# Loading keys and the first queries three gate sets earlier in a hybrid decoder layer

## The chip, the cores and the metric

The kernel runs on one core of a Trainium2 chip. The core has a matrix engine (TensorE, in the profile PE, its weight loads PEld), a vector engine (VectorE, DVE), a scalar engine (ScalarE, ACT), a general engine (GpSimd, POOL) and a synchronising engine (SyncE, SP), which here issues nearly all DMA transfers. Each engine works through its own list of instructions in order and waits by semaphores for the others. The metric is the device time of one execution in microseconds (us); lower is better.

## The reference, cut to what matters

One decoder layer over 1024 tokens of width 1024 in float32: a SwiGLU block, a mixer and a second SwiGLU block. The change lies in the mixer:

```python
proj = u @ w_in[l]
(nq, nkc, nvc, nks, nvs, nkw, nvw, ngt, rq, rk, rv, rg, ga, gb) = jnp.split(proj, split_pts, axis=-1)
o_nsa = nsa_attention(nq..., nkc, nvc, nks, nvs, nkw, nvw, jax.nn.sigmoid(ngt)..., cmp_k_pe[l], cmp_k_w1[l], ...)
o_ret = retention(rq..., rk..., rv..., pos)
...
mixed = jax.nn.sigmoid(ga) * y_nsa + jax.nn.sigmoid(gb) * y_ret
# inside nsa_attention: kc = compress(k_cmp, ...), vc = compress(v_cmp, ...); for every head
# softmax of q @ kc (compressed), q @ k_slc (selected) and q @ k_win (window), each times its values, summed by gates
def compress(raw, pe, w1, w2):
    ...
    return jax.nn.silu(flat @ w1) @ w2
```

So there are projections of the normed input `u` (queries, keys, values, two wide gates `ga` and `gb`), a small network that compresses keys and values, a recurrent "retention", and an attention with three branches.

## The kernel before, in words

**Precision.** Every float32 operand of a matmul is split into a high part (a cast on ACT) and a low part (a subtraction on DVE), and a product is three matmuls (`mm3`).

**Projections.** The wide projections are taken two column blocks at a time as a "set" (`set_t`): `wset` (lines 321 to 348) loads two weight tiles `raw` of 512 KB, called a and b here, into the pool `W`, which holds **three** `raw` tiles in this stage; GpSimd forms sums and differences S of them (lines 341 to 344), ACT and DVE split them into `wp` (lines 334 and 335), and `seven` (line 380) runs seven products of 12 matmuls of 128x512 (line 281). The moving operands of the seven products are, in this order, u0, u0, T2, T3, T4, u1, u1 (in the profile u0h/u0l, t2h/t2l and so on), tiles of the pool `sp`. The results are added on DVE (lines 395 to 416), and for the gates ACT applies the sigmoid (line 1453) and SP stores them in DRAM (`d_gab`).

There are eleven such sets in `sets()`: keys (to `d_k`), two of queries (to `d_q`, one slab for each of four pairs of heads), and eight gate sets, called gate set 0 to gate set 7 below. They are one generator, `fill`, woven in the program into the retention core, the compression and the key loading. A planner of the tile framework then orders the instructions of each engine by its own costs, so that the order in the program is a wish, not the result.

**Compression** (`compress`, lines 822 to 879) runs for keys and then for values. For each: DMA of the raw rows into `kst`, the weights `w1` and the position rows `pe`; a transpose of `pe` (line 840); its copy (842); a chain of 16 dependent DVE instructions on `pea` (844, 846); one small matmul (848) and the copy of its result as bias (851); 16 matmuls over `kst` (855, 32 records in the trace); the activation `hid` (859); a second small matmul (873 for the values); and the splits into `v2c` (878, 879). `kst` is one place, so the rows of the values come when the matmuls of the keys are done.

**Keys and queries.** `keys` (line 1010) loads `d_k` back in four parts, each two DMAs of 256 KB (line 1020) into a stage tile that is one of the **same three** `raw` tiles, and splits it into `Kh` (ACT, line 1022) and `Kl` (DVE, line 1023). These live in a pool `kv`, which takes the room of the pool that the compression used. `queries(p)` does the same with `d_q[p]` in two halves (lines 1048, 1049, 1050). The queries of pair 0 go to the place `t3h`, which the moving operand T3 of the sets has until the last set's fourth product; those of pair 1 go to `t3l`, over a stage tile `t4h` that lies where T4 was.

**Attention** (line 1067). For each pair and each block of 128 queries PE makes score tiles (lines 1063 and 1064), DVE adds the mask and takes the row minimum (1110 to 1122), ACT takes the exponential (1125), GpSimd scales (1130), and so on.

The program's order around the change, in `run`, is: last of the retention, compression woven with four steps of `fill` for each of its own, then `fill` up to the mark "late", then `keys` with two steps of `fill` after each part, then the rest of `fill`, then queries of pair 0, values, queries of pair 1, attention.

Of the kernel before, what the change touches and what calls it, by code (L numbers as in the profile page):

```python
# [10 lines left out]
F32R = mybir.dt.float32r  # L11
# [6 lines left out]
P = 128  # L18
T = 1024
D = 1024  # L20
KD = D // P
# [12 lines left out]
def drain(*gens):  # L34
    for g in gens:
        for _ in g:
            pass


def weave(main, fill, n):  # L40

    done = 0
    for i, _ in enumerate(main, 1):
        while done < i * n:
            next(fill, None)
            done += 1


def f32(ap):
    return ap.bitcast(F32)  # L50


class Layer:
# [953 lines left out]
    def stage(self):  # L1007
        return self.W.tile([P, 2, H2], F32, name="raw", bufs=self.wr)
# [30 lines left out]
    def queries(self, p, pool, stage):  # L1039
        nc = self.nc  # L1040
        src = self.d_q[p].rearrange("(j d) t -> d j t", j=2)
        Q = self.Q[p] = pool.tile([P, 2, T], F32R, name="t3" + "hl"[p % 2])
        lr = slice(64, 128) if p < 2 else slice(0, 64)
        for hf in (1, 0):
            s = slice(hf * H2, (hf + 1) * H2)
            a = stage()
            for r in range(2):
                nc.sync.dma_start(a[64 * r:64 * r + 64], src[:, :, s])
            nc.scalar.copy(Q[:, :, s], a)
            nc.vector.tensor_sub(Q[lr, :, s], a[lr], f32(Q[lr, :, s]))  # L1050

    def scores(self, ps, h, b, i, k0, kn, off):

        nc = self.nc
        g = h // 4
        e = slice(i * P, (i + 1) * P)
        q = self.Q[h // 2][:, h % 2, e]
        a = off
        while a < off + kn:
            z = min(off + kn, (a // H2 + 1) * H2)  # L1060
            ks = slice(k0 + a - off, k0 + z - off)
            kh, kl = (self.kch, self.kcl) if b == 2 else (self.Kh[b], self.Kl[b])
            nc.tensor.matmul(ps[:, a:z], q, kh[:, g, ks], start=True, stop=False)  # L1063
            nc.tensor.matmul(ps[:, a:z], q, kl[:, g, ks], start=False, stop=True)  # L1064
            a = z

    def attention(self, pool, sp, stage, psS, psT, psO, fill):
# [7 lines left out]
        for p in range(4):  # L1075
            g = p // 2
            for i in range(NT - 1, -1, -1):
                if p and p < 3 and i == 7:
                    self.queries(p + 1, sp, stage)
                elif i in FILL[p]:  # L1080
                    next(fill, None)
                late = p == 3 and i < 4
# [205 lines left out]
    def run(self):  # L1288
# [6 lines left out]
        def pool(ctx, name, side="left"):  # L1295
            return ctx.enter_context(tc.tile_pool(name=name, bufs=1, side=side, reuse_waits="tile"))

        def psum(ctx, name, bufs):
            return ctx.enter_context(tc.tile_pool(name=name, bufs=bufs, space=PSUM, reuse_waits="tile"))
# [133 lines left out]
        sp = pool(c_n, "sevenm", "right")  # L1433
# [12 lines left out]
        def to(dst):  # L1446
            def sink(n, hf, t):
                nc.sync.dma_start(dst[n][:, hf * H2:(hf + 1) * H2], t)
            return sink

        def to_gate(d):
            def sink(n, hf, t):
                nc.scalar.activation(t, t, AF.Sigmoid)
                nc.sync.dma_start(self.d_gab[d + (KD if n == "b" else 0), :, hf * H2:(hf + 1) * H2], t)
            return sink
# [19 lines left out]
        def sets():  # L1475
            yield from self.set_t(self.w_in, 768, 1024, us, sp, to({"a": self.d_k[0], "b": self.d_k[1]}))
            for p in (0, 2):
                yield from self.set_t(self.w_in, p * P, (p + 1) * P, us, sp, to({"a": self.d_q[p], "b": self.d_q[p + 1]}))
            for d in range(KD):
                if d == KD - 1:  # L1480
                    yield "late"
                yield from self.set_t(self.w_in, 3352 + d * P, 4376 + d * P, us, sp, to_gate(d))

        drain(sets_ret(0))
        more = sets_ret(1)
        fill = itertools.chain(more, sets())
        for r in range(2):
            with ExitStack() as c1:
# [4 lines left out]
        kv = pool(c_n, "kv", "right")  # L1493
        for x in fill:
            if x == "late":
                break
        weave(self.keys(kv), fill, 2)
        drain(fill)


        c_ps.close()
        c_a = ExitStack()
        psT, psS, psO = psum(c_a, "psT", 3), psum(c_a, "psS", 4), psum(c_a, "psOT", 1)
        self.Q = {}
        self.queries(0, sp, self.stage)
        self.values(sp, self.stage)
        self.c_w.close()

        def stage():
            return sp.tile([P, 2, H2], F32, name="t4h")  # L1510
        att = pool(c_a, "att")
        self.queries(1, sp, stage)
        onsa = self.attention(att, sp, stage, psS, psT, psO, self.ret_up(sp, stage, psS))
        c_a.close()
        c_n.close()
# [76 lines left out]
```

## Time and profile before

| | us |
|---|---|
| Three runs | 2452.97, 2454.83, 2447.19; median 2452.97 |
| The profiled execution | 2450.27, of which span of the trace 2448.5 |
| Gate set 6 begins on PE | 1223.98 |
| Last matmul of gate set 7 starts | 1271.63 |
| First score tile reduced on DVE | 1283.81 |
| First exponential of the attention on ACT | 1289.90 |
| Mean granted clock of TensorE | 0.967 of full speed |

The times within the span count from its start. A row of the list of instructions in order of time gives the start, the duration, the engine, the line of the kernel, the operation and its tiles, the shape, how many instructions are merged in the row (x), and in brackets how long the engine had been idle and what released it.

### The profile page before, as it was taken

Reading aid. Unit: us, or ns where it says so; the run is one execution under the profiler, and the core shown is the slowest. Engines: PE = TensorE matmul, PEld = TensorE weight load, DVE = VectorE, ACT = ScalarE, POOL = GpSimd, SP = SyncE. Lnnn points to the kernel's source line nnn. Section 1 sums busy time; section 2 is a strip of 40 time slices with the busy share of each in tenths; the row PEclk is TensorE's granted clock in tenths of the full one; section 3 lists DMA queues with packets and bytes.
Section 4 is the critical chain, followed back from the end, with each engine's and each line's share of the span. In section 5 each row is a group of like instructions: output and inputs, shape, how many; then the busy total and the mean of one; then the engine's idle time right before and its main releaser. Section 6 shows DMA issues by size and latency. Waiting matters only on the chain.

```text
span 2448.5 us, 32717 instructions
## 1 busy us (share of the span) xinstructions
PE 2284.3 (93%) x11563; PEld 1909.0 (78%) x11563; DVE 1860.7 (76%) x2790; ACT 1031.7 (42%) x1860; POOL 1252.7 (51%) x920
## 2 busy tenths in 40 slices
PE   7799999999977999999989999988889999999997
PEld 5578888878856899888868889866668888887875
DVE  8888887578999856666668887669985555558998
ACT  5333222245744422223348776624432222235655
POOL 3855454444576545555215544456754444435366
PEclk8999999999998999999998999999889999999998
DMA  9135655263204344343551221640322222255201
GB/s 345 56 112 169 201 176 186 86 232 134 78 0 136 97 142 121 110 138 110 167 165 51 74 79 57 213 153 0 103 69 78 82 78 86 85 190 186 94 1 69
DMA packets 248888, 288.32 MB, mean 118 GB/s; under 512 B 14852, under 2 KB 169236, under 8 KB 248724
## 3 DMA queue, kind: packets, MB, share of 16 engines
q1 hardware_dynamic: 248608, 286.19, 36.6%
q8 instruction: 91, 1.49, 0.3%
q14 instruction: 73, 0.60, 0.1%
q10 hardware_dynamic: 116, 0.05, 0.0%
HBM read 216.45 MB, written 69.73 MB: 117 GB/s over the span
## 4 chain that ended last, share of the span: by engine, by line
PE 31%; DVE 12%; DMA 3%; issue 2%; ACT 1%; POOL 1%; SPq 0%; DVEq 0%; ACTq 0%; POOLq 0%
PE po L281 16%; DVE wp L678 4%; PE ot L1166 2%; DVE hT L782 2%; PE po L750 2%; PE pt L1152 2%; PE s L750 2%; PE s L281 2%; PE s L1063 1%; PE s L1064 1%; DMA tn<-d_gab 1%; PE pt L855 1%; PE ot L1163 0%; PE po L495 0%; DMA hT<-d_h 0%
## 5 line engine op out<-in xcount | busy, mean ns | idle before, releaser
L750 PE MATMUL po<-wp 128*128 128x512 f32 x1176 | 293.7, 406 | 30.2 <-DVE wp L678 27.6
L281 PE MATMUL po<-u0h,wp 128*128 128x512 f32 x944 | 305.6, 395 | 9.2 <-DVE gates L991 4.9
L750 PEld LDWEIGHTS po<-wp 128*128 128x128 f32 x1176 | 227.9, 196 | 91.2 <-DVE wp L678 38.1
L281 PE MATMUL po<-u1h,wp 128*128 128x512 f32 x880 | 281.9, 391 | 3.7 <-DVE bias L544 2.2
L750 PE MATMUL s<-wp 128*128 128x512 f32 x1008 | 247.4, 403 | 21.0 <-DVE wp L678 19.7
L750 PEld LDWEIGHTS s<-wp 128*128 128x128 f32 x1008 | 195.9, 195 | 67.3 <-DVE wp L678 24.4
L334 ACT CAST wp<-S 128x1024 fp32r<-128x1024 f32 x98 | 102.9, 1050 | 302.5 <-PE po L281 300.4
L281 PEld LDWEIGHTS po<-u0h,wp 128*128 128x128 f32 x944 | 178.9, 189 | 49.9 <-DVE gates L991 5.1
L463 POOL TENSOR_TENSOR t<-t,t 128x512 f32<-128x512 f32 x38 | 55.3, 1456 | 301.8 <-DVE t L407 191.9
L281 PEld LDWEIGHTS po<-u1h,wp 128*128 128x128 f32 x880 | 165.1, 188 | 40.5 <-DVE bias L544 2.6
L281 PE MATMUL po<-u0l,wp 128*128 128x512 f32 x472 | 185.4, 393 | 0.0
L281 PE MATMUL po<-u1l,wp 128*128 128x512 f32 x440 | 172.5, 392 | 2.6 <-DVE u1l L243 2.6
L335 DVE TENSOR_TENSOR wp<-S,wp 128x1024 fp32r<-128x1024 f32 x98 | 159.8, 1630 | 15.8 <-ACT wp L334 15.6
L334 ACT CAST wp<-raw 128x1024 fp32r<-128x1024 f32 x98 | 82.0, 837 | 186.0 <-PE po L281 174.4
L341 POOL TENSOR_TENSOR S<-raw 128x512 f32<-128x512 f32 x49 | 68.7, 1403 | 157.0 <-DMA raw<-w_in 92.2
L281 PE MATMUL po<-t2h,wp 128*128 128x512 f32 x392 | 132.2, 397 | 2.2 <-ACT t2h L300 2.1
L281 PE MATMUL po<-t3h,wp 128*128 128x512 f32 x392 | 132.1, 398 | 0.2 <-DVE t L395 0.2
L281 PE MATMUL po<-t4h,wp 128*128 128x512 f32 x392 | 131.6, 396 | 0.8 <-DVE tn L399 0.7
L395 DVE TENSOR_TENSOR t<-tn,po 128x512 f32<-128x512 f32 x57 | 39.0, 685 | 110.4 <-issue 78.7
L335 DVE TENSOR_TENSOR wp<-raw,wp 128x1024 fp32r<-128x1024 f32 x98 | 113.6, 1159 | 11.9 <-ACT wp L334 11.8
L1156 DVE TENSOR_TENSOR pl<-pt,ph 128x512 fp32r<-128x512 f32 (+2 forms) x160 | 96.9, 619 | 11.9 <-ACT ph L1155 11.1
L281 PEld LDWEIGHTS po<-u0l,wp 128*128 128x128 f32 x472 | 89.7, 190 | 18.1
(471 smaller groups left out, 6248.4 us busy)
## 6 DMA issues: line engine op xcount, KB each, us to landing
raw<-ffn_w_in SPq DMA_DIRECT2D x88, 512.0 KB, 4.8
raw<-ada_w SPq DMA_DIRECT2D x56, 512.0 KB, 4.4
raw<-w_in SPq DMA_DIRECT2D x40, 512.0 KB, 4.2
d_g<-t SPq DMA_DIRECT2D x50, 256.0 KB, 2.0
d_h<-hT SPq DMA_DIRECT2D x24, 512.0 KB, 5.8
hT<-d_h SPq DMA_DIRECT2D x48, 256.0 KB, 5.3
d_g<-tg SPq DMA_DIRECT2D x38, 256.0 KB, 2.0
fw<-ada_w SPq DMA_DIRECT2D x8, 1024.0 KB, 11.1
```

The source lines that it names most:

```text
L281: nc.tensor.matmul(ps, a, b, start=k == 0 and q == 0, stop=k == n - 1 and q == 2)
L334: nc.scalar.copy(w[:, 0], t)
L335: nc.vector.tensor_sub(w[:, 1], t, f32(w[:, 0]))
L341: nc.gpsimd.tensor_add(s[:, 0:4], b[:, 0:4], b[:, 4:8])
L395: nc.vector.tensor_add(c, u2, p)
L463: nc.gpsimd.tensor_mul(g, g, t)
L678: nc.vector.tensor_sub(w[:, x, 1], g(n[x]), f32(w[:, x, 0]))
L750: nc.tensor.matmul(po[d], l[:, e], r, start=k == 0 and z == 0 and not seeded, stop=k == m - 1 and z == 2, skip_group_check=seeded)
L782: self.nc.vector.scalar_tensor_tensor(h, po, self.ab[:, 3 * i + 2, d:d + 1], h, op0=ALU.mult, op1=ALU.add)
L1152: nc.tensor.transpose(pt[:, o + j * P:o + (j + 1) * P], a, self.ident)
L1156: nc.vector.tensor_sub(lo, pt[:, :n], f32(hi))
L1166: nc.tensor.matmul(ot, self.V2[kt // 4][:, kt % 4, b, g, :], x[:, o:o + 2 * P], start=first and m == 0, stop=last and m == 1)
```

## The change

The tile of pair 0's queries gets a name of its own, `Q0`, and is taken from the pool `kv` beside the keys. `queries` becomes a generator with a step after each half; where it was called before it is now drained. `keys` and these queries are chained and woven, two steps of `fill` each time, from a mark "late" that stands before gate set 5 instead of gate set 7.

```diff
     def queries(self, p, pool, stage):
         nc = self.nc
         src = self.d_q[p].rearrange("(j d) t -> d j t", j=2)
-        Q = self.Q[p] = pool.tile([P, 2, T], F32R, name="t3" + "hl"[p % 2])
+        Q = self.Q[p] = pool.tile([P, 2, T], F32R, name="t3" + "hl"[p % 2] if p else "Q0")
...
             nc.scalar.copy(Q[:, :, s], a)
             nc.vector.tensor_sub(Q[lr, :, s], a[lr], f32(Q[lr, :, s]))
+            yield
...
                 if p and p < 3 and i == 7:
-                    self.queries(p + 1, sp, stage)
+                    drain(self.queries(p + 1, sp, stage))
...
             for d in range(KD):
-                if d == KD - 1:
+                if d == KD - 3:
                     yield "late"
...
-        weave(self.keys(kv), fill, 2)
+        self.Q = {}
+        weave(itertools.chain(self.keys(kv), self.queries(0, kv, self.stage)), fill, 2)
         drain(fill)
...
         psT, psS, psO = psum(c_a, "psT", 3), psum(c_a, "psS", 4), psum(c_a, "psOT", 1)
-        self.Q = {}
-        self.queries(0, sp, self.stage)
         self.values(sp, self.stage)
...
-        self.queries(1, sp, stage)
+        drain(self.queries(1, sp, stage))
```

What the planner makes of it is seen in the order of the built programs. First TensorE, where gate set 5 ends (its last product is on u1). Before, gate set 6 (u0) follows at once, and the four steps of the values' compression (lines 840, 848, 855 and 873) stand far apart among the matmuls of gate sets 6 and 7:

```order
L281 MATMUL po<-u1l,wp 128x512
L281 MATMUL po<-u1h,wp 128x512
L281 MATMUL po<-u0h,wp 128x512
L281 MATMUL po<-u0l,wp 128x512
L281 MATMUL po<-u0h,wp 128x512 x2
```

Now the four stand together between gate set 5 and gate set 6:

```order
L281 MATMUL po<-u1l,wp 128x512
L281 MATMUL po<-u1h,wp 128x512
L840 MATMUL pt<-ident,pe 128x16
L848 MATMUL pt<-ones,pea 128x1
L855 MATMUL pt<-kst,w_9561 128x126 x16
L873 MATMUL pt<-w_9563,hid 64x64 x2
L281 MATMUL po<-u0h,wp 128x512
```

Nothing of gate set 6 is left ahead of them. After the two u0 products of gate set 6 come eight score matmuls of the attention's first block, then the rest of gate sets 6 and 7, then the attention.

VectorE at the same place: before, the chain of the values' compression (`pea`) is spread over gate set 6, between additions (lines 399 to 412) and weight splits (335), and the key splits (1023) come at the end of gate set 7:

```order
L844 TENSOR_SCALAR pea<-w_9561,peT 128x128
L846 SCALAR_TENSOR_TENSOR pea<-w_9561,peT,pea 128x128 x3
L399 TENSOR_TENSOR tn<-tn,po 128x512
L846 SCALAR_TENSOR_TENSOR pea<-w_9561,peT,pea 128x128 x5
L403 TENSOR_TENSOR tg<-tn,po 128x512
L846 SCALAR_TENSOR_TENSOR pea<-w_9561,peT,pea 128x128 x5
L407 TENSOR_TENSOR t_10271<-tg,po 128x512
```

Now it is one piece behind gate set 5's last addition (416), the key splits follow it, and the first weight split of gate set 6 (335) comes after all of them:

```order
L416 TENSOR_TENSOR tn<-tn,po 128x512
L842 COPY peT<-pt 128x16
L844 TENSOR_SCALAR pea<-w_9561,peT 128x128
L846 SCALAR_TENSOR_TENSOR pea<-w_9561,peT,pea 128x128 x15
L851 COPY peb<-pt 128x1
L879 TENSOR_TENSOR v2c<-pt,v2c 64x64
L1023 TENSOR_TENSOR Kl_10044<-raw,Kh_10042 128x2x512 x2
L1023 TENSOR_TENSOR Kl_10045<-raw,Kh_10043 128x2x512
L879 TENSOR_TENSOR v2c<-pt,v2c 64x64 x2
L1023 TENSOR_TENSOR Kl_10045<-raw,Kh_10043 128x2x512
L879 TENSOR_TENSOR v2c<-pt,v2c 64x64
L335 TENSOR_TENSOR wp<-raw,wp 128x1024
```

SyncE, which issues the loads: before, the two weight tiles of gate set 7 (line 327) go out between stores of the gates, and the later parts of the keys (1020) follow them:

```order
L327 DMA raw<-w_in 128x8x128
L1454 DMA d_gab<-tg 128x512
L1454 DMA d_gab<-tn 128x512
L327 DMA raw<-w_in 128x8x128
L1454 DMA d_gab<-t_10225 128x512
L1454 DMA d_gab<-t_10271 128x512
L1020 DMA raw<-d_k 64x2x512 x2
```

Now the last part of the keys goes out first, then the two weight tiles of gate set 6, then both halves of pair 0's queries (1048), then the two weight tiles of gate set 7:

```order
L1455 DMA d_gab<-tn 128x512
L1020 DMA raw<-d_k 64x2x512 x2
L327 DMA raw<-w_in 128x8x128 x2
L1048 DMA raw<-d_q 64x2x512 x4
L327 DMA raw<-w_in 128x8x128 x2
L1455 DMA d_gab<-t_10255 128x512
```

All of these go into the three `raw` places. In the built program the two weight tiles of gate set 6 take the places of the second and third parts of the keys, the last part of the keys takes the place of the first, and both halves of the queries follow in that place. The queries of pair 0 and the keys share the order on ACT: the casts of `Kh` stand behind the values' `hid` (859) and the first `v2c` (878). In the pool `kv`, which has grown by `Q0`, the high parts of the first keys now lie outside the room of the compression; their low parts lie where `kst` and the keys' `w1` were.

## Rows read from the trace of the kernel before

**Rows 1.** The page, busy time, share of the span and instructions by engine:

```profile
PE 2284.3 (93%) x11563; PEld 1909.0 (78%) x11563; DVE 1860.7 (76%) x2790; ACT 1031.7 (42%) x1860; POOL 1252.7 (51%) x920
```

**Rows 2.** TensorE in order of time, from gate set 6 into the attention:

```profile
1223.98 0.39 PE L281 MATMUL po<-u0h,wp 128*128 128x512 f32 x1
...
1242.12 0.50 PE L281 MATMUL po<-u1h,wp 128*128 128x512 f32 x1 [1.25 <-DVE t L407]
...
1244.98 0.28 PE L848 MATMUL pt<-ones,pea 128*128 128x1 f32 x2
...
1250.30 7.04 PE L855 MATMUL pt<-kst,w 128*128 128x126 f32 x32
...
1260.47 0.45 PE L873 MATMUL pt<-w,hid 128*64 128x64 f32 x4
...
1271.63 0.39 PE L281 MATMUL po<-u1h,wp 128*128 128x512 f32 x1
1273.81 0.50 PE L1063 MATMUL s<-Kh,t3h 128*128 128x512 f32 x1 [1.79 <-DVE t3h L1050]
...
1284.55 0.79 PE L1063 MATMUL s<-Kh,t3h 128*128 128x512 f32 x1 [8.96 <-DVE mx L1110]
```

**Rows 3.** Stretches of TensorE: from:to and length, busy (instructions), granted clock, DMA:

```profile
1276.00:1278.00 2.00, 0.00 (x0) 1.00 1.15 213
1278.00:1280.00 2.00, 0.00 (x0) 0.76 1.11 333
...
1290.00:1292.00 2.00, 1.38 (x4) 0.50 0.47 160
...
1296.00:1298.00 2.00, 2.00 (x13) 0.98 0.00 0
```

**Rows 4.** VectorE in order of time, both compressions, key splits and attention's start:

```profile
1189.39 1.51 DVE L846 SCALAR_TENSOR_TENSOR pea<-w,peT,pea 128x128 f32<-128x128 f32 x4
...
1224.18 0.69 DVE L416 TENSOR_TENSOR tn<-tn,po 128x512 f32<-128x512 f32 x1 [0.47 <-PE po L281]
...
1230.28 0.17 DVE L842 COPY peT<-pt 128x16 f32<-128x16 f32 x1
...
1230.97 0.28 DVE L844 TENSOR_SCALAR pea<-w,peT 128x128 f32<-128x128 f32 x1
...
1236.07 5.39 DVE L846 SCALAR_TENSOR_TENSOR pea<-w,peT,pea 128x128 f32<-128x128 f32 x5
...
1262.14 2.36 DVE L1023 TENSOR_TENSOR Kl<-raw,Kh 128x1024 fp32r<-128x1024 f32 x2 [0.73 <-ACT Kh L1022]
...
1283.81 0.68 DVE L1110 CUSTOM_DVE_ANT_0 u0h<-s,S 128x512 f32<-128x512 f32 x1
```

**Rows 5.** ScalarE in order of time, from the values' compression to the first exponential:

```profile
1257.38 0.37 ACT L859 ACTIVATE hid<-pt,peb 128x126 f32<-128x126 f32 x1 [7.25 <-PE pt L855]
...
1260.95 0.21 ACT L878 CAST v2c<-pt 64x64 fp32r<-64x64 f32 x1 [0.51 <-PE pt L873]
...
1265.41 1.05 ACT L1022 CAST Kh<-raw 128x1024 fp32r<-128x1024 f32 x1 [2.12 <-DMA raw<-d_k]
...
1287.54 1.04 ACT L1049 CAST t3l<-t4h 128x1024 fp32r<-128x1024 f32 x1 [5.28 <-DMA t4h<-d_q]
1288.60 1.28 ACT L1125 ACT_TABLE_LOAD   x1
1289.90 1.15 ACT L1125 ACTIVATE u0h<-u0h,mx 128x1024 f32<-128x1024 f32 x1
```

**Rows 6.** First key load on SP; DMA issues (count, KB, median us to landing); landing of stage t4h:

```profile
1206.05 0.65 SPq L1020 DMA_DIRECT2D raw<-d_k  x1
...
raw<-d_k SPq DMA_DIRECT2D x8, 256.0 KB, 4.5
...
raw<-w_in SPq DMA_DIRECT2D x40, 512.0 KB, 4.2
...
DMA to landing us min/median/max: 3.3/4.5/7.5
```

## The prediction

> **What bounds the kernel now.** I read the page first: TensorE is busy for 93% of the span [rows 1], so a gain has to close a hole on it or shorten what stands ahead of one. Then I read the instructions of TensorE in order of time around the place that the change touches [rows 2]. Gate sets 6 and 7 run from 1223.98 to about 1271.9 (the last matmul starts at 1271.63 and the next could follow 0.23 later). Then TensorE waits 1.79 us for pair 0's queries, makes the first four score tiles in about 1.7 us, and waits 8.96 us for VectorE, whose first score reduction is at 1283.81 [rows 2, 4]. The first exponential is at 1289.90, behind the split of pair 1's queries and a table load of 1.28 us [rows 5]. That is 18.0 us from the end of gate set 7 to the first exponential. The granted clock shows the same hole: it falls from 1.00 to 0.50 of 2.4 GHz within some 4 us of the last score tile, and is back only in the stretch from 1296 [rows 3]. This hole is what the change can win; 18 us minus what has to be done there anyway.
>
> The other thing to read is why the keys were late before. The first key load is issued at 1206.05 [rows 6], but its cast begins after 1260.95, behind the first `v2c` of the values' compression [rows 5]. So it was not the load that the keys waited for, but the compression: the places of the keys lie in its room, and on ACT their casts stand behind its `hid` and `v2c`.
>
> **The change, part by part: the compression on TensorE.** Now look at the order of the built program. Nothing of gate set 6 stands ahead of the values' compression any more, and nothing can: the weight tiles of gate set 6 take `raw` places that the second and third key parts hold, these are free only when the keys are split, the splits stand on VectorE behind `pea` and the first `v2c`, and on ACT behind `hid`. So TensorE, done with gate set 5 at 1223.98, goes through one dependent chain. I add it up from rows:
>
> 1. Last addition of gate set 5, copy, first step: 0.69 + 0.17 + 0.28 [rows 4]; then 15 steps on `pea`. These took 1.51 for 4 (0.38 each) in one place and 5.39 for 5 (1.08 each) in another [rows 4]; in the second GpSimd was forming S of the next weights. Now these weights are not loaded, GpSimd has nothing to do, so I take 0.38: 5.7. Bounds 5.7 and 16. Together 6.8.
> 2. Matmul 848, bias copy (about 0.15), 855, `hid`, 873, first `v2c`: 0.28 + 0.15 + 7.04 + 0.37 + 0.45 + 0.21 [rows 2, 5] = 8.5.
> 3. The clock: TensorE has stood for 6 us by then, longer than it stood when the clock fell [rows 3]. It was at half from the restart near 1290.6 until 1296 [rows 3], about 5 us, which is 2.5 us of work lost. I add 2.5; bounds 0 and 2.7.
> 4. Key cast 1.05, two low parts 2.36 [rows 4, 5]: 3.4. Now the place for weight tile a of gate set 6 is free.
> 5. Weight tile a: issue 0.4, landing 4.2 [rows 6], cast 1.05, thus 5.7. But the last key part takes longer, and its low part stands ahead of the weight split on VectorE: it can be issued one low part (1.2) earlier, its two issues cost about 1.2, then landing 4.5 [rows 6], cast 1.05, split 1.2, thus 6.8 from the end of step 4. Then the `v2c` split 0.2 and the weight split 1.2. Together 8.2.
>
> The sum is 29.4 us from the end of gate set 5 to the start of gate set 6. Of this, 8.0 us of TensorE work (840, 848, 855, 873) lay inside gate sets 6 and 7 before, and the wait of 1.25 us there for VectorE [rows 2], which was busy with `pea`, should go. So gate set 6 proper starts **20 us later** than it would have.
>
> **Gate sets 6 and 7.** The 14 products took (1271.9 - 1223.98 - 8.0 - 1.25) / 14 = 2.76 us each; that stays. The restart costs another 2.5 us at half clock, and the eight score matmuls that now stand inside gate set 6 cost 1.7 us. They need the first half of pair 0's queries, which goes into the place of the last key part: free at 29.4 - 1.4 = 28 after gate set 5, plus issue 1.2, landing 4.5 and two splits 2.3 = 36. TensorE gets there after 29.4 + 5.5 + 2.5 = 37.4: no wait, with 1 us to spare. The weights of gate set 7 go out behind the second half of the queries, near 38 to 42, and are wanted at about 52: covered, with 5 us to spare after the landing and the split. So gate set 7 ends near 1271.9 + 20.1 + 2.5 + 1.7 = **1296.2**, some 24 us later.
>
> **The start of the attention.** Pair 0's queries and the keys are then ready, and the 1.79 us wait and the crowd of loads (DMA share 1.11 in [rows 3]) go. What is late next is pair 1's queries: their stage `t4h` lies on T4, so their load still waits for gate set 7's fifth product, 5.5 us before the end. From there: issue 0.6, landing 4.5 [rows 6], cast 1.05, split 1.2, then the second half 0.6 + 4.5 + 1.05 (same rows), and the table load 1.28 [rows 5]: 14.8, so 9.3 us after the end of gate set 7 instead of 18.0. This gives back 8.7. The first exponential comes at 1305.5, **15.6 us later** than 1289.90. VectorE has by then reduced eight score tiles instead of five, worth about 1.5 us where it is the later one; That TensorE then works at full clock for the next 6 us I take at nothing (bounds -2 and 0), because each score tile of that stretch also waits for VectorE. Net: 24.3 - 8.7 - 1.5 = **+14 us**.
>
> **Costed at nothing.** `Q0` as a place, the `drain` calls and the steps of the generator add no instruction. The second weight tile of gate set 5 is loaded one turn later, but its split waited for a `wp` place anyway; if that cover fails it costs 1 to 3 us at gate set 5. The planner also orders the first pair of the attention anew; nothing is added there, and I give it -3 to +3.
>
> **A rule against this.** The key load issued at 1206.05 was used 55 us later [rows 5, 6]. The Trainium skill, page "DMA: Bandwidth & Descriptors", section "Rules for kernel authors", says to issue a DMA early, compute meanwhile and wait for it late, so that its fixed cost is hidden. By that rule alone loading keys and queries sooner wins the hole before the attention; here the early load holds one of three places that weights need, which the rule doesn't speak of. It is the second rival below.
>
> **The rivals.**
> - *Slower by 9 to 20 us* (forecast): the chain above.
> - *Faster*: the keys are out of the way before gate set 6 needs its places, the weights come in time, and the hole goes: 1.79 + 8.96 us and half of the slow stretch, about -13, thus 2440. For it: that is what the order in the program asks for, and the high parts of the first keys lie outside the compression's room now. Against it: ACT and VectorE have these splits behind `hid`, `v2c` and `pea` in their lists, and the low parts lie on `kst`. It would need gate set 6's weights landed within 8 us of gate set 5's end; the chain makes that 23.
> - *No difference*: the chain is right but every uncertain term is at its lower end: no clock loss twice (-5), landings at 3.3 (-3), the attention's new order at its best (-3): +3, thus 2456. It decides where the hole in TensorE is under 22 us instead of 29.
> - *Much slower*, over +20: `pea` at the slow rate (+10), or gate set 7's weights, behind two query halves on SP, late as well: their 5 us to spare is used up if each of three loads takes 2 us longer than the median; then +6 to +10. Thus 2474 to 2480.
>
> **How the numbers follow.** The sum is made against the profiled execution: 2450.27 + 14 = 2464.3. That execution is 2.7 below the median of the three runs, 2452.97, against which a new median would be held; so I predict 2467. The chances: forecast 0.70, no difference 0.13, much slower 0.09, faster 0.08. The range from 2456 to 2477 takes in the forecast, the upper part of no difference, and the lower part of much slower; about 2 in 10 is left out. About 0.3%, or 7.4 us, is what a measurement of this kernel tells from no change. Faster by more than that: 0.08; within it: 0.13 and a little of the forecast's lower end, 0.15; slower: 0.77.
>
> **What the profile of the changed kernel would show.** Right: TensorE stands for about 6 us before 848 and for 10 us or more between 873 and gate set 6; 855 and the start of gate set 6 run at a clock of 0.50; the last matmul of gate set 7 starts near 1296; the first exponential comes about 9 us after it, behind the split of pair 1's queries. Wrong: gate set 6 beginning before 1245, key splits ahead of 855, or a wait at gate set 7's first product. The prediction falls if the hole ahead of gate set 6 is less than 15 us, or if the attention gains much more than 9 us at its start.

## The result, and the profile after

| | kernel before | changed kernel |
|---|---|---|
| First comparison, median of 5 runs each | 2452.97 us | 2463.68 us (2461.49 to 2469.24) |
| The same kernels again beside e10 (11 and 6 runs) | 2450.23 us | 2464.44 us (2461.43 to 2473.16) |
| Ratio, with 95% interval | 1 | 1.0055 (1.0041 to 1.0069); again 1.0065 (1.0047 to 1.0083) |
| Profiled execution, and its span | 2450.27, 2448.5 | 2461.49, 2459.7; again 2467.15, 2465.3 |

The change makes the kernel slower, by 10.7 us in the first comparison and by 14.2 us in the second; 14 was forecast. The page shows that nothing was added: each engine is busy within 2 us of what it was [rows 1].

```profile
PE 2285.0 (93%) x11563; PEld 1909.2 (78%) x11563; DVE 1861.6 (76%) x2790; ACT 1031.6 (42%) x1860; POOL 1251.0 (51%) x920
```

So it is time in which TensorE stands. Its instructions in order of time (start, duration, what it is; in brackets the idle time ahead and what ended it), which answer to [rows 2]:

```profile
1199.67 0.50 PE L281 MATMUL po<-u0h,wp 128*128 128x512 f32 x1 [2.19 <-DVE tn L416]
...
1225.57 0.23 PE L840 MATMUL pt<-ident,pe 16*128 16x16 f32 x1
1232.63 0.58 PE L848 MATMUL pt<-ones,pea 128*128 128x1 f32 x2 [6.84 <-DVE pea L846]
1233.46 7.20 PE L855 MATMUL pt<-kst,w 128*128 128x126 f32 x32 [0.25 <-DVE peb L851]
1241.12 0.45 PE L873 MATMUL pt<-w,hid 128*64 128x64 f32 x4 [0.46 <-ACT hid L859]
1252.78 0.79 PE L281 MATMUL po<-u0h,wp 128*128 128x512 f32 x1 [11.21 <-ACT wp L334]
1260.87 0.39 PE L1064 MATMUL s<-Kh,Q 128*128 128x512 f32 x1
...
1294.81 0.39 PE L281 MATMUL po<-u1h,wp 128*128 128x512 f32 x1
1298.31 0.50 PE L1064 MATMUL s<-Kh,Q 128*128 128x512 f32 x1 [3.12 <-DVE mx L1111]
```

Gate set 5 ends at 1225.57, gate set 6 begins at 1252.78: 27.2 us, with waits of 6.84 and 11.21 us. The hole ahead of the attention is won: the wait for the first reductions is 3.12 us where it was 8.96, and the one of 1.79 us for pair 0's queries is gone.

VectorE and ScalarE in order of time, which answer to [rows 4, 5]:

```profile
1226.80 5.78 DVE L846 SCALAR_TENSOR_TENSOR pea<-w,peT,pea 128x128 f32<-128x128 f32 x15
...
1242.79 3.50 DVE L1023 TENSOR_TENSOR Kl<-raw,Kh 128x1024 fp32r<-128x1024 f32 x3 [0.73 <-ACT Kh L1022]
...
1250.16 1.22 DVE L1023 TENSOR_TENSOR Kl<-raw,Kh 128x1024 fp32r<-128x1024 f32 x1 [3.14 <-ACT Kh L1022]
```

```profile
1251.68 1.04 ACT L334 CAST wp<-raw 128x1024 fp32r<-128x1024 f32 x1 [1.33 <-DMA raw<-w_in]
...
1301.73 1.04 ACT L1049 CAST t3l<-t4h 128x1024 fp32r<-128x1024 f32 x1 [3.42 <-DMA t4h<-d_q]
1302.79 1.28 ACT L1126 ACT_TABLE_LOAD   x1
1304.09 1.15 ACT L1126 ACTIVATE u0h<-u0h,mx 128x1024 f32<-128x1024 f32 x1
```

SP between them, the last key part and then both weight tiles of gate set 6:

```profile
1244.04 1.24 SPq L1020 DMA_DIRECT2D raw<-d_k  x2
1245.37 1.33 SPq L327 DMA_DIRECT2D raw<-w_in  x2
```

Read them as one chain: `pea`, the compression on TensorE, the low parts of the keys (three from 1242.79, some 1.2 us each), behind the first of them the last key part's load and behind the second the weights' load at 1245.37, then the cast of gate set 6's first weights, which waits for its DMA. At the attention's start the split of pair 1's queries and the table load stand ahead of the first exponential, 9.0 us after the end of gate set 7 (1294.81 + 0.23), where it was 18.0.

Executions differ by some us outside the change as well. So I also compare one stretch, from the fourth sum of gate set 4 (an addition of line 403, still before any difference on TensorE) to the last addition of the attention. VectorE, kernel before and then the changed one:

```profile
1188.26 0.69 DVE L403 TENSOR_TENSOR tg<-tn,po 128x512 f32<-128x512 f32 x1 [2.03 <-PE po L281]
...
1573.02 0.58 DVE L1173 TENSOR_TENSOR t<-ot,t 64x128 f32<-64x128 f32 x2 [1.78 <-ACT t L1171]
```

```profile
1186.23 0.69 DVE L403 TENSOR_TENSOR tg<-tn,po 128x512 f32<-128x512 f32 x1 [2.03 <-PE po L281]
...
1586.25 0.58 DVE L1174 TENSOR_TENSOR t<-ot,t 64x128 f32<-64x128 f32 x2 [1.78 <-ACT t L1172]
```

The stretch took 384.76 us before and 400.02 after, **+15.3**. Up to the first exponential it is +16.2 (1304.09 - 1186.23 against 1289.90 - 1188.26). In the whole span only 11.2 of that are left: this execution entered the stretch 2.0 us ahead, and made up another 2.0 behind it, in parts that the edit doesn't touch. The second execution of the changed kernel (e9) did not.

### The profile page after: what moved, and what is told of

Its sections match the earlier page's. It is cut to its first block, busy times and chain, and to the rows that moved or that the text cites. A ratio compares the mean times of both kernels' runs of the same rounds, so it can differ in the third digit from the quotient of the medians.

```text
span 2459.7 us, 32706 instructions
## 1 busy us (share of the span) xinstructions
PE 2285.0 (93%) x11563; PEld 1909.2 (78%) x11563; DVE 1861.6 (76%) x2790; ACT 1031.6 (42%) x1860; POOL 1251.0 (51%) x920
## 4 chain that ended last, share of the span: by engine, by line
PE 34%; DVE 12%; DMA 3%; issue 2%; ACT 2%; POOL 2%; SPq 0%; DVEq 0%; ACTq 0%; POOLq 0%
PE po L281 19%; DVE wp L678 4%; PE po L750 2%; PE ot L1167 2%; DVE hT L782 2%; PE s L750 2%; PE pt L1153 2%; PE s L281 2%; PE s L1064 1%; PE s L1065 1%; DMA tn<-d_gab 1%; DMA t4h<-d_q 1%; PE pt L855 1%; DMA raw<-w_in 0%; PE po L495 0%
## 5 line engine op out<-in xcount | busy, mean ns | idle before, releaser
L281 PE MATMUL po<-u0h,wp 128*128 128x512 f32 x944 | 309.2, 398 | 21.4 <-ACT wp L334 11.2
```

The costliest lines, as they stand in the source:

```text
L281: nc.tensor.matmul(ps, a, b, start=k == 0 and q == 0, stop=k == n - 1 and q == 2)
```

## The experiments

Theory A is that of the prediction: the key parts hold the `raw` places that gate set 6's weights need, and are freed only behind the values' compression. Each kernel was compared with runs of the kernel before on the same chip; "stretch" is the stretch above in its profiled execution, against that of the kernel before.

| run | median, kernel before beside it (us) | ratio, 95% interval | to the first exponential | stretch |
|---|---|---|---|---|
| e1 keys early alone | 2467.24, 2449.36 | 1.0072 (1.0058 to 1.0086) | +15.5 | +15.6 |
| e2 queries' place alone | 2451.01, 2449.36 | 1.0002 (0.9994 to 1.0011) | +0.7 | 0.0 |
| e3 keys early, own stage | 2444.52, 2449.36 | 0.9984 (0.9975 to 0.9993) | -3.5 | -4.8 |
| e4 and pair 1 through it | 2445.57, 2449.36 | 0.9992 (0.9983 to 1.0000) | -3.5 | -8.7 |
| e5 mark one set later | 2459.38, 2450.38 | 1.0041 (1.0029 to 1.0053) | +6.3 | +8.2 |
| e6 shorter `pea` | 2460.11, 2450.38 | 1.0044 (1.0032 to 1.0056) | +11.1 | +11.4 |
| e7 e4, casts in order | 2446.01, 2450.38 | 0.9980 (0.9972 to 0.9988) | -8.5 | -14.5 |
| e8 hole filled | 2466.41, 2450.38 | 1.0070 (1.0057 to 1.0083) | +17.4 | +18.9 |
| e9 changed kernel again | 2464.44, 2450.23 | 1.0065 (1.0047 to 1.0083) | +14.5 | +13.5 |
| e10 four raw places | 2456.98, 2450.23 | 1.0031 (1.0019 to 1.0043) | +10.1 | +10.0 |

**The two halves of the change: e1 and e2.** In e1 only the mark of the kernel before is moved (the diff); in e2 only the queries' place and weave are changed, with the mark at KD - 1.

```diff
-                if d == KD - 1:
+                if d == KD - 3:
```

> The keys alone are woven three gate sets ahead; pair 0's queries stay where they were, in the place t3h and after gate set 7, so one half of the change is undone. Theory A (the key parts hold the raw places that gate set 6's weights need, and are freed only behind the values' compression): TensorE has the same hole ahead of gate set 6, which starts near 1252, about 20 us later than in the kernel before without its compression inside, and none of the hole at the attention's start is won but what the queries gain from a quieter SP: 18 us from the end of gate set 7 to the first exponential become 13 to 18. Sum 20 + 2.5 (half clock) - 0 to 5: +17 to +23 us against the kernel before, ratio 1.007 to 1.0095. Rival B (the loss comes from the queries: their loads ahead of gate set 7's weights, or their place): without them the keys cost nothing, gate set 6 follows gate set 5 at once, within 3 us of the kernel before. Rival C (the early work on ScalarE and VectorE itself costs, wherever it is staged): about half of the +10.7 us, +4 to +7.

> Pair 0's queries have their own place and are woven behind the keys, but the mark stands at gate set 7 as in the kernel before: the other half of the change. Theory A: gate set 6 has its weights in time, no hole ahead of it (TensorE's order there is that of the kernel before); the wait of 1.79 us for pair 0's queries goes if their loads land before gate set 7 ends, but they stand behind the keys on SP as before, and pair 1's queries still come through the place of T4: 0 to -5 us, ratio 0.998 to 1.000. Rival B (queries cost): +5 us or more, with a wait at gate set 7's first product. Rival C: no more than 2 us either way.

Measured: e1 +17.9 us at the medians and +15.6 in the stretch, e2 no difference. TensorE in e1, and the first exponential on ScalarE:

```profile
1252.52 0.80 PE L281 MATMUL po<-u0h,wp 128*128 128x512 f32 x1 [10.37 <-ACT wp L334]
...
1294.51 0.39 PE L281 MATMUL po<-u1h,wp 128*128 128x512 f32 x1
```

```profile
1303.88 1.15 ACT L1125 ACTIVATE u0h<-u0h,mx 128x1024 f32<-128x1024 f32 x1
```

The hole is that of the changed kernel, so the early keys alone make it; rival B falls. The first exponential comes 9.1 us after gate set 7 here too, sooner than the 13 to 18 that I expected, though the queries are still in `t3h`. What the change wins at the attention's start it wins with the keys, not with the queries' place, as e2 says from the other side. The medians of e1 and of the changed kernel differ, but their intervals overlap.

**The same early keys, another place: e3.** The stage of the keys is a pool of its own, three tiles beside `kv` in room that is free without `Q0`; the mark stands at KD - 3.

```diff
-        weave(self.keys(kv), fill, 2)
+        c_k = ExitStack()
+        kp = pool(c_k, "ks", "right")
+        def own():
+            return kp.tile([P, 2, H2], F32, name="ks", bufs=3)
+        weave(self.keys(kv, own), fill, 2)
```

> The keys are loaded and split three gate sets ahead as in the changed kernel, but through three stage places of their own (12 KB a partition that the pool kv without Q0 leaves free) in place of the three raw places; pair 0's queries stay in t3h. Theory A: with nothing held, gate set 6 follows gate set 5 at once (1224 to 1226, clock 1.00), the values' compression lies inside gate sets 6 and 7 as before, the keys are split there too, and gate set 7 ends near 1272; then the crowd of loads ahead of the attention is smaller, the first exponential comes about 9 us after gate set 7's end, where the kernel before has 18: -6 to -10 us, about 2444 us, ratio 0.996 to 0.9975. Rival C (the early splits themselves stand in the way of the weights, wherever they are staged): the hole ahead of gate set 6 stays at over 15 us and the time is that of the changed kernel or more, +8 to +20. A third reading, that the hole is won but the attention's start is bound by something else than the loads: within 3 us of the kernel before.

A stretch of e3 behind gate set 5 (from:to and length, busy and instructions of each engine, granted clock, DMA), then its instructions and ScalarE's:

```profile
1224.00:1226.00 2.00, 2.00 (x10) 1.67 (x9) 1.55 (x3) 1.48 (x3) 0.00 (x0) 1.00 1.17 328
```

```profile
1248.03 7.04 PE L855 MATMUL pt<-kst,w 128*128 128x126 f32 x32
...
1270.12 0.39 PE L281 MATMUL po<-u1h,wp 128*128 128x512 f32 x1
```

```profile
1258.79 2.95 ACT L1022 CAST Kh<-ks 128x1024 fp32r<-128x1024 f32 x3
...
1281.79 1.04 ACT L1049 CAST t3l<-t4h 128x1024 fp32r<-128x1024 f32 x1 [5.18 <-DMA t4h<-d_q]
...
1284.15 1.15 ACT L1125 ACTIVATE u0h<-u0h,mx 128x1024 f32<-128x1024 f32 x1
```

There is no hole and no clock loss: TensorE is busy for 2.00 of 2.00 us, the compression lies inside gate sets 6 and 7 again, and the keys, whose first load goes out at 1020.3, are still split only behind it, at 1258.79. So early loads by themselves do no harm; 22.7 us lie between e1 and e3 (2467.24 and 2444.52), and the stage is the one difference between them. Theory A stands, and rival C, by which the hole stays wherever the keys are staged, falls. Whether splits that are also done early would cost something is not shown: in every run here they come behind the compression's `hid`. The size was missed, -4.8 instead of -6 to -10: the first exponential comes 13.8 us after gate set 7, not 9, since the second half of pair 1's queries waits 5.18 us for its load into `t4h`.

**What is late next: e4 and e7.** In e4 pair 1's queries go through the new stage; in e7 the casts of the retention's result are kept in the program's order besides (the second part of the diff).

```diff
+        self.queries(1, sp, own)
-        self.queries(1, sp, stage)
...
-        nc.scalar.copy(o[0][:, k, :], a)
+        self.tc.keep_in_program_order(nc.scalar.copy(o[0][:, k, :], a))
```

> As the run with a stage of its own for the keys, and pair 1's queries go through that stage too instead of through t4h, so they no longer wait for gate set 7's fifth product. Theory A, with pair 1's queries as what is late next at the attention's start (named so in the prediction): the first exponential comes 4 to 7 us after gate set 7's end, another 3 to 5 us won against the run without this edit: -9 to -14 us, 2440 us, ratio 0.994 to 0.9965. If pair 1's queries are not what is late next: the same time as the run without this edit, within 2 us. Rival C: as there, +8 to +20.

> The kernel with a stage of its own for keys and pair 1's queries, and the casts of the retention's result (u1h from t4h) are kept in the order of the program on ScalarE, behind the first block's exponentials. In the run without this edit the first exponential waited until 1288.6 behind such a cast, which waited 6.6 us for its load into t4h, while its scores had been reduced by about 1281.5. If that wait is what stands there: the first exponential about 1.3 us (table load) behind its last reduction, near 1283, 5 to 6 us earlier, and the whole -6 to -9 us against the kernel before, ratio 0.9963 to 0.9976. If VectorE bounds the first block there anyway: the same as the runs with their own stage, -2 to -5 us, ratio 0.998 to 0.999.

ScalarE in e4, then TensorE in e7 behind the attention and one stretch of it:

```profile
1274.34 1.05 ACT L1049 CAST t3l<-ks 128x1024 fp32r<-128x1024 f32 x1 [1.71 <-DMA ks<-d_q]
...
1286.27 1.05 ACT L1191 CAST u1h<-t4h 128x1024 fp32r<-128x1024 f32 x1 [6.60 <-DMA t4h<-d_ret]
```

```profile
1564.84 0.79 PE L281 MATMUL po<-u0h,wp 128*128 128x512 f32 x1 [3.88 <-ACT wp L260]
...
1587.04 0.77 PE L281 MATMUL po<-u0h,wp 128*128 128x512 f32 x1 [3.85 <-DVE tn L1233]
```

```profile
1580.00:1600.00 20.00, 16.15 (x61) 12.82 (x60) 4.64 (x7) 1.24 (x2) 6.36 (x5) 0.83 0.99 320
```

e4 as a whole is barely faster, -3.8 us at the medians with 1.0000 still in the interval, instead of the expected -9 to -14. Pair 1's queries are ready near 1277, but another load into `t4h` stands ahead of the first exponential: the planner had put a cast of the retention's result there. e7 takes it away, and counted from the start of the stretch the first exponential comes 8.5 us sooner than before, the end of the attention 14.5 us. Of this only 4.4 us are left in the medians of the whole kernel: the profiled execution of e7 entered the stretch 2.9 us late and lost 8.2 us behind it. In the merge behind the attention TensorE waits twice for almost 4 us, for weights and for gate products, where these waits were 2.29 and 1.09 in the kernel before, and its clock in the 20 us shown is 0.83 (1.00 before, 1580 to 1600). The DMA engines are busy for 0.99 of that time, as they were before (1.02). So what comes sooner seems to run into loads that don't; this was not tried by itself. So e7's expected -6 to -9 was missed too, and e3 and e7 (about -4.5 us) are the versions that beat both kernels.

**The length of the chain: e6.** The changed kernel without 12 of the 15 steps on `pea` for the values.

```diff
-            for o in range(1, 16):
+            for o in range(1, 4 if b else 16):
```

> The changed kernel without 12 of the 15 chained steps on pea for the values (so the position rows' share in their compression is left out in part). Theory A: these steps stand one behind the other in the hole at 0.385 us each, so gate set 6 starts 4.6 us earlier, as does all that follows: +6 us against the kernel before where the changed kernel has +10.7, ratio 1.0020 to 1.0030; the hole ahead of 848 falls from 6.8 to 2.2 us, and TensorE may keep its clock over it. If the hole is set by the landing of the weights or by loads on SP and not by this chain: no change against the changed kernel, ratio 1.0044.

TensorE in e6:

```profile
1228.66 0.59 PE L848 MATMUL pt<-ones,pea 128*128 128x1 f32 x2 [2.19 <-DVE pea L846]
...
1248.07 0.80 PE L281 MATMUL po<-u0h,wp 128*128 128x512 f32 x1 [10.48 <-ACT wp L334]
```

The wait ahead of 848 is 4.65 us shorter. Counted from the end of gate set 5, gate set 6 starts 4.7 to 5.4 us sooner than in the changed kernel's two executions, and the first exponential, counted from the start of the stretch, 3.4 to 5.2 us sooner. The chain is serial, step for step. The whole time doesn't show it well: +9.7 us, against +10.7 and +14.2, too close to tell apart, and the expected +6 (up to 1.0030) lies below its interval.

**One set later: e5.** The mark at KD - 2.

> The changed kernel with the mark one gate set later, before gate set 6. Theory A (the raw places): the weights of gate set 6 come in time, those of gate set 7 wait for key parts, whose splits stand behind the values' bias copy, 855, hid, 873 and v2c. The chain on pea runs beside gate set 6, so the hole stands ahead of gate set 7 and is shorter than the 27.2 us of the changed kernel by its 6.6 us for pea: about 20.6 us, of which 8.0 are compression work that lay in gate sets 6 and 7 before; plus 2.5 for the restart at half clock, minus the 9 us won at the attention's start: +4 to +8 us against the kernel before, ratio 1.0015 to 1.003. Rival C (the early work itself costs in proportion to how early it is): two thirds of the changed kernel's loss, +7. If the weights were not held, -6 to -10 as in the run with a stage of its own.

TensorE in e5, at the start of gate set 7:

```profile
1252.40 0.45 PE L873 MATMUL pt<-w,hid 128*64 128x64 f32 x4 [0.46 <-ACT hid L859]
1263.68 0.79 PE L281 MATMUL po<-u0h,wp 128*128 128x512 f32 x1 [10.83 <-ACT wp L334]
```

As theory A has it, the hole moves to gate set 7 with the mark. It is somewhat dearer than I had worked out, +8.2 in the stretch and +9.0 at the medians instead of +4 to +8. Gate set 7 has two waits for VectorE, 0.70 and 1.52 us, that the sum left out (the kernel before has one of 1.25); what makes up the rest is not shown. The whole time alone would also fit rival C's +7; the place of the hole does not.

**A fourth place: e10**, beside the changed kernel again, **e9**.

```diff
-WF, WM = (4, 4), (3, 3)
+WF, WM = (4, 4), (3, 4)
```

> The changed kernel with four raw places instead of three. Theory A (places held until the values' compression is done): a fourth place is taken by the fourth key part, so gate set 6's weights still go out only when the first parts are split, and the hole ahead of gate set 6 stays; but gate set 5's second tile no longer waits behind the first key part (3.5 us in the changed kernel: a wait of 2.19 and 1.3 at half clock), and the last key part is not loaded and split inside the hole, so the weights go out about 1.3 us earlier and land sooner: 4 to 6 us less than the changed kernel, +4 to +7 against the kernel before, ratio 1.0017 to 1.0029. If it were merely one place too few (a rival within A: any spare place lets the weights in): no hole, -6 to -10. If places had nothing to do with it: +10.

> The changed kernel once more, unedited, beside the run with a fourth raw place. By its first runs +8 to +13 us against the kernel before (ratio 1.0055, interval 1.0041 to 1.0069). In the profile the stretch that the change touches, from the last sets before gate set 5 to the end of the attention, should again be 15 us longer than in the kernel before, whatever the stretches outside it do; if that was chance of one execution, it comes out 3 us or more away from 15.

SP in e10, then TensorE:

```profile
1172.96 0.38 SPq L327 DMA_DIRECT2D raw<-w_in  x1
...
1240.66 1.51 SPq L327 DMA_DIRECT2D raw<-w_in  x2
```

```profile
1229.26 0.59 PE L848 MATMUL pt<-ones,pea 128*128 128x1 f32 x2 [6.84 <-DVE pea L846]
...
1245.83 0.80 PE L281 MATMUL po<-u0h,wp 128*128 128x512 f32 x1 [7.64 <-ACT wp L334]
```

A fourth place is simply held by a fourth key part: gate set 6's weights still go out only behind the first splits, at 1240.66, and the hole stays. Its second wait is 2.8 to 3.6 us shorter than in the changed kernel's two executions (10.48 and 11.21), as expected of a last key part that is no longer loaded inside it. The wait in gate set 5 is gone. At the medians +6.8 us, as expected. e9 gave +14.2 at the medians and +13.5 in the stretch.

**The clock: e8.** The changed kernel with 62 unused matmuls behind 873.

```diff
+                for m in range(62):
+                    nc.tensor.matmul(pc[:, P:H2], u[0][:, m % 8, 0:P], u[1][:, m % 8, 0:H2 - P], start=True, stop=True)
```

> The changed kernel with 62 more matmuls of 128x384 right behind 873, which fill TensorE's idle time of some 10.5 us ahead of gate set 6 with products that nothing uses. They are to tell what the clock of 0.50 at gate set 6's start costs: there 24 matmuls took 8.3 us in the changed kernel where 5.5 is their time at full clock. If the clock is kept over the hole, gate set 6's two u0 products take 5.5 us and all that follows comes 2.7 us earlier: +8 us against the kernel before, ratio 1.0028 to 1.0040; the planner also moves the casts of the keys ahead of v2c here, worth up to 1 us. If the half clock isn't what the 2.7 us come from, or the other 0.50 stretch behind 848 matters: the changed kernel's +10.7. If the added matmuls outlast the hole, more than that by what they outlast it, up to 3 us.

TensorE in e8, instructions and stretches:

```profile
1242.92 11.04 PE L876 MATMUL pt<-u1l,u1h 128*128 128x384 f32 x62
1253.79 0.39 PE L281 MATMUL po<-u0h,wp 128*128 128x512 f32 x1
...
1261.92 0.79 PE L281 MATMUL po<-t2h,wp 128*128 128x512 f32 x1 [2.49 <-ACT tn L391]
```

```profile
1255.00:1257.00 2.00, 2.00 (x10) 1.64 (x9) 0.00 (x0) 0.39 (x1) 2.00 (x2) 1.00 0.18 39
...
1262.00:1266.00 4.00, 4.00 (x11) 3.19 (x12) 2.31 (x5) 1.86 (x4) 0.00 (x0) 0.59 1.11 249
```

The u0 products of gate set 6 ran at 1.00 and took 5.6 us (to 1261.92 - 2.49) instead of 8.1, the last one's end included, so the price of the half clock there is confirmed. The edit as a whole lost, though, +16.0 us where +8 was expected. The cast of gate set 6's first weights was done at 1252.57, but the added matmuls ran until gate set 6 began at 1253.79; they held up the values' `v2c` casts on ScalarE, the copy of the first product stood behind those, TensorE waited 2.49 us for it, and then the clock was 0.59.

## Why the prediction was right, step by step

The direction, the mechanism and the forecast of +14 held: 10.7 and 14.2 at the medians, 15.3 and 13.5 in the stretch. Two errors of opposite sign, +3.6 and -2.2 us, stand inside the sum, so that it came this close is in part luck:

- **Costed at nothing, and wrong: gate set 5's second weight tile.** I let the `wp` place cover its later load, at 1 to 3 us if that failed. It failed, for 3.6 us: gate set 5 ended 39.3 us after the addition that opens the stretch instead of 35.7. SP, before and then after, and GpSimd after:

```profile
1174.30 0.38 SPq L327 DMA_DIRECT2D raw<-w_in  x1
```

```profile
1165.07 1.32 SPq L1020 DMA_DIRECT2D raw<-d_k  x2
1172.27 0.39 SPq L327 DMA_DIRECT2D raw<-w_in  x1
1186.68 0.38 SPq L327 DMA_DIRECT2D raw<-w_in  x1
```

```profile
1192.67 1.30 POOL L341 TENSOR_TENSOR S<-raw 128x512 f32<-128x512 f32 x1 [28.28 <-DMA raw<-w_in]
```

  The first key part took the turn, the second tile went out at 1186.68 instead of 1174.30, and GpSimd's S, then the split, then VectorE's last addition of gate set 4 were late: TensorE waited 2.19 us and then ran at 0.50. In e9 the wait was 2.22 us, the clock stayed at 1.00, and gate set 5 ended 2.1 us later than in the kernel before.
- **The chain: 29.4 forecast, 27.2 measured.** Steps 1, 2 and 4 with 5 came out at 7.1, 9.2 and 11.0 us (forecast 6.8, 8.5 and 11.6), which makes 27.2 and includes the gaps between engines in step 2 that I had left out. `pea` ran at the lower of its two bounds, 5.78 us, with GpSimd idle (1197.9 to 1253.4), as I had assumed. The term that was mis-sized is step 3, the clock: 855 began at 0.50, as I said it would, but it took only 0.16 us longer than before and 848 only 0.30, where the sum has 2.5.
- Gate set 6's start at half clock (+2.5, measured 8.1 - 5.4 = 2.7), the score matmuls (1.7), no wait for pair 0's queries, gate set 7's weights covered: all as worked out. Counted from the start of the stretch, gate set 7 ended 25.2 us later, forecast 24.3.
- The attention's start: 9.0 us to the first exponential, forecast 9.3, and for the reason given, pair 1's queries through T4's place. That the gain comes with the queries' place I had not claimed, and e1 and e2 show that it doesn't.
- The forecast -1.5 behind the first exponential was -0.9 (+16.2 to +15.3).

Of the rivals, *faster* fell as argued: the splits stood behind the compression in every kernel, e3 too. *No difference* fell with the interval of 1.0041 to 1.0069 and a hole of 27.2 us, *much slower* with `pea` at its fast rate and gate set 7's weights in time. The Trainium skill, page "DMA: Bandwidth & Descriptors", section "Rules for kernel authors", says to issue a DMA early and wait for it late. Both sides of that are now measured: with a stage of its own the early load is worth 4.8 us (e3), in a place that others wait for it costs 10.7 to 14.2, or 17.9 for the keys alone (e1).

## What to carry to other kernels

Ask of an early load not when its data could be there but when its place comes free again, and who is next in that place; if its consumer stands behind a long chain, the chain is moved onto whoever wants the place, and one more shared place was only held in turn (e10). A small place of its own made the same edit a gain here. And a gain early in a kernel has to be followed to its end: of the 14.5 us that e7's profiled execution won in the stretch, 8.2 were lost behind it.

## What the hardware showed that I had not expected

**The half clock hardly slowed the matmuls of line 855** (7.20 us, the first 4 of them at 0.50, where they took 7.04). Stretches of the changed kernel, first two inside 855, then two in gate set 6:

```profile
1234.00:1236.00 2.00, 2.00 (x12) 2.00 (x11) 0.00 (x0) 0.77 (x1) 0.00 (x0) 0.50 0.04 8
1238.00:1240.00 2.00, 2.00 (x11) 1.92 (x10) 0.00 (x0) 0.00 (x0) 0.00 (x0) 1.00 0.00 0
1254.00:1256.00 2.00, 2.00 (x6) 1.51 (x6) 0.00 (x0) 0.00 (x0) 2.00 (x2) 0.50 0.47 101
1258.00:1260.00 2.00, 2.00 (x10) 1.60 (x9) 1.97 (x2) 1.40 (x3) 1.82 (x1) 0.95 0.00 0
```

At 1.2 GHz 855's instructions of 128x126 go on at 12 in 2 us, at 2.4 GHz at 11; those of 128x512 fall from 10 to 6. In the two stretches of 855 the weight loads of TensorE (PEld) fill the time, 2.00 and 1.92 of 2.00 us, at a median of 0.206 us each; in those of 128x512 they don't (1.51 and 1.60). That the weight loads set the pace at either clock agrees with the rows but was not tried alone. The Trainium skill, page "TensorE: Matmul & The Clock Gate", section "Back-to-back issue gap", says that in a stream of weight loads, each with its matmul, the spacing is set by both instructions; these rows agree. So a loss to the clock has to be costed by the instruction's shape, not by the busy time.

**Waits of about 2 us brought the clock down in some executions and not in others.** In gate set 5 of the changed kernel the clock was 0.50 behind a wait of 2.19 us, which made 3.6 us in all, and 0.59 behind one of 2.49 in e8; in the kernel before I had only seen it fall in a gap of 9 us. But at the same place of the same kernel, in e9, it stayed at 1.00:

```profile
1203.94 0.50 PE L281 MATMUL po<-u0h,wp 128*128 128x512 f32 x1 [2.22 <-DVE tn L416]
```

At that place it was also 1.00 behind 1.71 us in e8, but 0.50 behind 1.75 in e1 and 1.92 in e6. So the length of the wait alone did not decide it in these runs.
